# Hybrid attention encoder: gate units moved between the attentions, two scalings moved to ScalarE, four query buffers, half of each weight residual moved to GpSimd

## The chip, the cores and the metric

The kernel runs on one core of one Trainium2 chip. The metric is the device time of one execution in microseconds (us). Engines are named as in the profile: PE is TensorE's matmul side and PEld its weight load, DVE is VectorE, ACT is ScalarE, POOL is GpSimd, SP is SyncE, which here only issues DMAs.

## The reference

Two layers, each on 512 rows of 1024 numbers in float32:

```python
h = rmsnorm(x, norm_g[l])
proj = h @ w_in[l]                     # 1024 -> 4096 columns: q, k, v, gate of groups A and B
# group A, 8 heads x 64: attention in a window of 8 x 16 grid cells, learned relative bias
# group B, 4 heads, two score maps of 64 each, v of 128:
logits = einsum(q, k) * scale
p = softmax(logits + bias)             # bias: T5 buckets, the same in both layers
attn = p[:, :, 0] - lam * p[:, :, 1]
out = rmsnorm(attn @ v, subln_g) * (1 - lam_init)
# both groups
x = x + concat(out_a * silu(gate_a), out_b * silu(gate_b)) @ w_out[l]
```

A last RMSNorm closes the trunk.

## The kernel before

Every matrix product is computed in split precision. A float32 operand is held as a rounded high half and a residual, both in fp32r, and a product is three matmuls: high by high, high by low, low by high. The normalised activations stay resident as `hTh` and `hTl` (transposed, 1024 by 512).

Weights come in units of 256 columns: 24 input units per layer, then four output units. `load_unit` (L86) brings a unit in two halves of 512 KB over SP (L83), casts each half to `wh` on ACT (L98, 128x1024) and takes the residual `wl = raw - wh` in two instructions on DVE (L101, 128x512 each). The pool `wp` has two buffers of `wh` and of `wl`. When a unit is taken, the next one is converted, so the residual of unit n+1 goes into the buffer that the last matmul of unit n-1 frees.

The unit kinds are: V (`proj_tm`, L222, four PSUM tiles of 256 columns), Q (`proj_qk`, one PSUM tile of 512 columns for q, one for k), and G (`gates`, two PSUM tiles of 512 columns), each for group A or B: VB0-1, VA0-1, QB0-3, QA0-3, GB0-1, GA0-1. `evac_q` (L226) turns a q tile into two `qs` tiles (ACT L231, DVE L232), `evac_k` (L237) writes `kt` (ACT L245, DVE L246) and mirrors it to the other 64 partitions by a DMA (L247). A gate tile gives `th` on ACT (L252) and `u` on DVE (L254), and POOL multiplies it into `y` (L483).

AB0-3 are the attentions of group B (`attn_b`): for each of four row blocks two score tiles `st` (PE L271, L272), bias and minimum on DVE (L274), exp on ACT (L277), 1/z (L281, L282), two scalings (L283, L284), four transposes (L288), the split into `pth` and `ptl` (ACT L163, DVE L164), and for each pair of blocks twelve value matmuls (L293). Its tail squares and sums (L297 to L304), takes `row` from PSUM (DVE L306), and goes on POOL and its DMA queue through `ms`, `rs_d` and `rb` to the last product (L308 to L315). AA0-3 are those of group A, two heads each (`attn_a`): `st` (L325), L331 on DVE, exp L334 on ACT, 1/z L336, scaling L337, two transposes (L340), the split, eight value matmuls (L347), and L353, L354.

Three things tie these together. PSUM pools are small: three projection tiles `pp`, two `st`, two `pt`, one `pv`. Some SBUF buffers are shared by tag: `th` with `row`, `u` with `rb`, two buffers each. And each engine runs its instructions in one order, which the framework's scheduler fixes when the program is built, from the program order; that in turn is set by the tuple `ORDER` (L32). The output projection (L540) of a layer comes after all 24 units, starts from the `y` tiles of group B split by ACT and DVE (L516, `yTh`, `yTl`), and is followed by the residual sum and the next norm.

Of the kernel before, what the change touches and what calls it, by code (L numbers as in the profile page):

```python
# [27 lines left out]
W4_BUFS = 10  # L28
WARM = (7, 2)
WRAW_BUFS = 2  # L30
QK_BUFS = 2
ORDER = ("VB0", "QB0", "AB0", "QB1", "VB1", "AB1", "QB2", "AB2", "QB3", "AB3", "VA0", "QA0", "AA0",  # L32
         "QA1", "AA1", "VA1", "QA2", "AA2", "QA3", "AA3", "GB0", "GB1", "GA0", "GA1")
A_TILES = ((0, 1), (1, 1), (2, 1), (0, 3))
A_SLOT = ((0, 0, 256), (1, 1, 128), (2, 1, 128), (0, 1, 768))
A_PV = ((1, 0, 128), (3, 256, 128), (0, 0, 384), (2, 128, 128))
# [10 lines left out]
def hybrid_encoder(ctx: ExitStack, tc: tile.TileContext, x, norm_g, w_in, na_rpb,  # L47
# [18 lines left out]
    V, A, G, T = nc.vector, nc.scalar, nc.gpsimd, nc.tensor  # L66
# [14 lines left out]
    def load_raw(src, hf):  # L81
        r = wp.tile([P, 4, 256], F32, name="wraw", bufs=WRAW_BUFS)
        nc.sync.dma_start(out=r.rearrange("p k c -> p (k c)"), in_=src[hf])  # L83
        return r

    def load_unit(src, raws=None, spare=False):  # L86
        if spare:
            wh, wl = (qk.tile([P, 4, S], F32R, name="kt", bufs=2).rearrange("p k (a c) -> p (k a) c", a=2)
                      for _ in range(2))
        else:  # L90
            wh = wp.tile([P, KC, 256], F32R, name="wh")
            wl = wp.tile([P, KC, 256], F32R, name="wl")
# [165 lines left out]
    def attn_b(h, q, k, vt, yb, nlam, sg, yout):  # L258
        pv = ps_v.tile([P, S], F32, name="pv")
        for qp in range(2):  # L260
            pth_v = w4.tile([P, 4, 256], F32R, name="pth", tag="w4k")
            ptl_v = w4.tile([P, 4, 256], F32R, name="ptl", tag="w4k")
            for qi in range(2):
                qt = 2 * qp + qi
                e = w4.tile([P, 2, S], F32, name="w4k")
                mn = small.tile([P, 2], F32, name="mn")
                z = small.tile([P, 2], F32, name="z")
                for m in range(2):
                    st = ps_s.tile([P, S], F32, name="st")
                    kh, kl = k[m]  # L270
                    T.matmul(out=st, lhsT=q[m][:, qt * P:(qt + 1) * P], rhs=kh, start=True, stop=False)  # L271
                    T.matmul(out=st, lhsT=q[m][:, qt * P:(qt + 1) * P], rhs=kl, start=False, stop=True)  # L272
                    lt = work.tile([P, S], F32, name="lt", bufs=2)
                    V.tensor_tensor_reduce(out=lt, in0=st, in1=yb[:, 48 - 16 * qt:560 - 16 * qt],  # L274
                                           scale=-1.0, scalar=3e38, op0=ALU.add, op1=ALU.min,
                                           accum_out=mn[:, m:m + 1])
                    A.activation(out=e[:, m, :].rearrange("p (b r c) -> p b r c", r=ROWS, c=C8),  # L277
                                 in_=lt.rearrange("p (r b c) -> p b r c", r=ROWS, c=C8),
                                 func=AF.Exp, bias=mn[:, m:m + 1], scale=-1.0, accum_out=z[:, m:m + 1])
                rz = small.tile([P, 2], F32, name="rz")  # L280
                V.reciprocal(out=rz, in_=z)  # L281
                V.tensor_scalar_mul(rz[:, 1:2], rz[:, 1:2], nlam)  # L282
                V.tensor_scalar_mul(e[:, 0, :], e[:, 0, :], rz[:, 0:1])  # L283
                V.scalar_tensor_tensor(out=e[:, 0, :], in0=e[:, 1, :], scalar=rz[:, 1:2], in1=e[:, 0, :],  # L284
                                       op0=ALU.mult, op1=ALU.add)
                pt = ps_t.tile([P, 4, P], F32, name="pt")
                for kt in range(4):
                    T.transpose(out=pt[:, kt, :], in_=e[:, 0, kt * P:(kt + 1) * P], identity=ident)  # L288
                split(pt, pth_v[:, :, qi * P:(qi + 1) * P], ptl_v[:, :, qi * P:(qi + 1) * P])
            n = 0  # L290
            for kt in range(4):
                for vs, pp in ((0, pth_v), (0, ptl_v), (1, pth_v)):
                    T.matmul(out=pv[:, qp * 256:(qp + 1) * 256], lhsT=vt[:, kt, h % 2, vs, :], rhs=pp[:, kt, :],  # L293
                             start=(n == 0), stop=(n == 11))
                    n += 1
# [22 lines left out]
    def attn_a(l, hd, half, q, k, vt, s_out):  # L318
# [3 lines left out]
        for j, (k0, dk) in enumerate(A_TILES):  # L322
            st = ps_s.tile([P, S], F32, name="st")
            for i in range(2):
                T.matmul(out=st[:, 0:256], lhsT=q[:, j * P:(j + 1) * P],  # L325
                         rhs=k[i].rearrange("p (t c) -> p t c", c=P)[:, k0:k0 + dk + 1:dk, :],
                         start=(i == 0), stop=(i == 1))
            e = work.tile([P, 256], F32, name="ea", bufs=3)
            mn = small.tile([P, 1], F32, name="mna")
            i0 = (0, 4, 4, 8)[j]  # L330
            V.tensor_tensor_reduce(out=e, in0=st[:, 0:256],  # L331
                                   in1=ba[:, 64 * i0:64 * i0 + 256],
                                   scale=-1.0, scalar=3e38, op0=ALU.add, op1=ALU.min, accum_out=mn)
            A.activation(out=e, in_=e, func=AF.Exp, bias=mn, scale=-1.0, accum_out=z[:, j:j + 1])  # L334
            rz = small.tile([P, 1], F32, name="rza")
            V.reciprocal(out=rz, in_=z[:, j:j + 1])  # L336
            V.tensor_scalar_mul(e, e, rz)  # L337
            pt = ps_t.tile([P, 4, P], F32, name="pt")
            for i in range(2):
                T.transpose(out=pt[:, i, :], in_=e[:, i * P:(i + 1) * P], identity=ident)  # L340
            t0, sl, stp = A_SLOT[j]
            oh, ol = (_view(p, t0 * 256 + sl * P, [[stp, 2], [1, P]]) for p in ptt)
            split(pt[:, 0:2, :], oh, ol)
# [64 lines left out]
    kh = [hTh[:, i] for i in range(KC)]  # L408
# [48 lines left out]
    for l in range(DEPTH):  # L457
# [223 lines left out]
```

## Time and profile before

| | |
|---|---|
| median of 3 runs | 631.58 us (631.32 to 632.37) |
| profiled execution | 631.53 us, span 629.8 us, mean granted PE clock 0.977 |
| PE busy | 594.4 us (94%) |
| DVE busy | 427.0 us (68%) |
| ACT busy | 320.2 us (51%) |
| POOL busy | 73.6 us (12%) |

All rows come from the profiled execution. PE is busy nearly all the time, so the time is PE's work plus the stretches in which PE idles or runs at a lower clock. A table of busy time by stretch finds these; the timeline of PE and of DVE in such a stretch tells what PE waited for and what stood ahead of it.

### The profile page before, as it was taken

The numbers are of one execution on the slowest core, as the hardware profiler recorded it, in microseconds if no ns is written. First come the engines' busy times: TensorE is split into PE (matmuls) and PEld (weight loads), VectorE is DVE, ScalarE is ACT, GpSimd is POOL, SyncE is SP. The second block draws the span as 40 slices with busy tenths as digits, with TensorE's granted clock in tenths as the row PEclk, the third lists the DMA queues.
The fourth block names the chain that finished last, engine by engine and source line by source line (L and its number), as shares of the span: only waits on it lengthen the run. The fifth ranks groups of instructions, "written<-read, shape, count | busy, mean of one in ns | idle before, by whom it ended". The sixth has DMA issues, their size and how long they took to land.

```text
span 629.8 us, 9006 instructions
## 1 busy us (share of the span) xinstructions
PE 594.4 (94%) x3230; PEld 504.5 (80%) x3230; DVE 427.0 (68%) x1011; ACT 320.2 (51%) x672; POOL 73.6 (12%) x91
## 2 busy tenths in 40 slices
PE   9899995899989999999999999688998999999995
PEld 7888883788888888888898798577887888888883
DVE  2755667597887777754674576578788877777263
ACT  5433546374656555734254344635666556664232
POOL 4400000111022002200000000020101200111001
PEclk9999997989999999999999999979999999999998
DMA  6854232313533443453643533320335354226214
GB/s 233 150 187 119 86 101 85 102 47 104 139 93 117 126 137 120 137 176 132 202 134 100 163 91 99 103 68 1 85 100 143 106 154 125 93 68 206 95 67 134
DMA packets 25166, 74.48 MB, mean 118 GB/s; under 512 B 7329, under 2 KB 7329, under 8 KB 24098
## 3 DMA queue, kind: packets, MB, share of 16 engines
q1 hardware_dynamic: 23648, 71.51, 37.6%
q0 software_dynamic: 1472, 2.40, 2.3%
q8 instruction: 26, 0.43, 0.3%
q14 instruction: 18, 0.15, 0.1%
q10 hardware_dynamic: 2, 0.00, 0.0%
HBM read 60.23 MB, written 4.21 MB: 102 GB/s over the span
## 4 chain that ended last, share of the span: by engine, by line
PE 81%; DVE 10%; ACT 5%; issue 3%; POOL 0%; POOLq 0%; DVEq 0%; ACTq 0%
PE pp L210 39%; PE pp L540 11%; PE pp L222 11%; PE pv L293 3%; PE pv L347 2%; PE pt L340 2%; DVE lt L274 2%; DVE wl L101 2%; PE st L325 2%; PE st L271 2%; PE pv L540 2%; PE st L272 2%; PE pt L288 1%; PE pt L195 1%; PE pp L437 1%
## 5 line engine op out<-in xcount | busy, mean ns | idle before, releaser
L101 DVE TENSOR_TENSOR wl<-wraw,wh 128x512 fp32r<-128x512 f32 x148 | 93.5, 686 | 52.6 <-ACT wh L98 20.7
L98 ACT CAST wh<-wraw 128x1024 fp32r<-128x1024 f32 x74 | 74.3, 1048 | 67.4 <-PE pp L210 33.8
L210 PE MATMUL pp<-hTh,wl 128*128 128x512 f32 x384 | 106.1, 399 | 0.0
L210 PE MATMUL pp<-hTh,wh 128*128 128x512 f32 x384 | 102.3, 398 | 0.4 <-DVE kt L246 0.4
L210 PE MATMUL pp<-hTl,wh 128*128 128x512 f32 x384 | 102.6, 396 | 0.0
L210 PEld LDWEIGHTS pp<-hTl,wh 128*128 128x128 f32 x384 | 70.7, 188 | 14.9
L210 PEld LDWEIGHTS pp<-hTh,wh 128*128 128x128 f32 x384 | 69.7, 188 | 14.6 <-PE pt L288 0.9
L210 PEld LDWEIGHTS pp<-hTh,wl 128*128 128x128 f32 x384 | 70.1, 188 | 14.0
L163 ACT CAST pth<-pt 128x256 fp32r<-128x256 f32 (+1 forms) x96 | 42.3, 443 | 70.2 <-PE pt L288 47.5
L222 PE MATMUL pp<-wh,hTh 128*128 128x256 f32 x224 | 66.0, 295 | 7.4 <-DVE v L164 7.0
L164 DVE TENSOR_TENSOR ptl<-pt,pth 128x256 fp32r<-128x256 f32 (+1 forms) x96 | 48.6, 508 | 31.3 <-ACT pth L163 30.6
L222 PE MATMUL pp<-wh,hTl 128*128 128x256 f32 x224 | 65.4, 292 | 0.0
L222 PE MATMUL pp<-wl,hTh 128*128 128x256 f32 x224 | 65.1, 290 | 0.0
L222 PEld LDWEIGHTS pp<-wh,hTh 128*128 128x128 f32 x224 | 44.2, 197 | 10.4 <-DVE v L164 7.9
L277 ACT ACTIVATE w4k<-lt,mn 128x512 f32<-128x512 f32 x64 | 45.9, 721 | 5.4 <-DVE mn L274 5.1
L274 DVE CUSTOM_DVE_ANT_0 lt<-st,yb 128x512 f32<-128x512 f32 x64 | 43.1, 681 | 3.4 <-PE st L272 2.9
L331 DVE CUSTOM_DVE_ANT_0 ea<-st,ba 128x256 f32<-128x256 f32 x64 | 26.4, 419 | 27.3 <-PE pt L340 19.6
L222 PEld LDWEIGHTS pp<-wl,hTh 128*128 128x128 f32 x224 | 44.0, 196 | 0.6
L222 PEld LDWEIGHTS pp<-wh,hTl 128*128 128x128 f32 x224 | 43.9, 196 | 0.5
L271 PE MATMUL st<-kt,qs 128*128 128x512 f32 x64 | 29.1, 454 | 11.0 <-DVE mn L274 9.2
L483 POOL TENSOR_TENSOR y<-y,u 128x512 f32<-128x512 f32 x16 | 21.6, 1348 | 144.7 <-DVE u L254 122.2
L334 ACT ACTIVATE ea<-ea,mna 128x256 f32<-128x256 f32 x64 | 32.7, 513 | 9.7 <-DVE mna L331 8.2
(124 smaller groups left out, 1066.7 us busy)
## 6 DMA issues: line engine op xcount, KB each, us to landing
wraw<-in_w_in_dram SPq DMA_DIRECT2D x64, 512.0 KB, 4.0
kt<-kt SPq DMA_DIRECT2D x16, 512.0 KB, 4.4
wraw<-in_w_out_dram SPq DMA_DIRECT2D x16, 512.0 KB, 3.7
ba<-in_na_rpb_dram SPq DMA_DIRECT2D x16, 384.0 KB, 3.6
y<-in_x_dram SPq DMA_DIRECT2D x8, 512.0 KB, 4.5
yb<-in_t_table_dram SPq DMA_DIRECT2D x8, 280.0 KB, 2.8
rb<-rs_d POOLq DMA_DIRECT2D x8, 256.0 KB, 4.4
xs_d<-y SPq DMA_DIRECT2D x4, 512.0 KB, 4.3
```

The source lines that it names most:

```text
L98: A.copy(out=wh[:, ks, :], in_=r)
L101: V.tensor_tensor(out=wl[:, kh, :], in0=r[:, 2 * i:2 * i + 2, :], in1=wh[:, kh, :].bitcast(F32), op=ALU.subtract)
L163: A.copy(out=oh, in_=ps)
L164: V.tensor_tensor(out=ol, in0=ps, in1=oh.bitcast(F32), op=ALU.subtract)
L210: T.matmul(out=pp, lhsT=a[:, kc, cs], rhs=b[:, kc, c0:c0 + S], start=(n == 0), stop=(n == 3 * KC - 1))
L222: T.matmul(out=pp[:, 0:256], lhsT=a[kc][:, c0:c0 + P], rhs=b[:, kc, :], start=(n == 0), stop=(n == 3 * KC - 1))
L271: T.matmul(out=st, lhsT=q[m][:, qt * P:(qt + 1) * P], rhs=kh, start=True, stop=False)
L274: V.tensor_tensor_reduce(out=lt, in0=st, in1=yb[:, 48 - 16 * qt:560 - 16 * qt], scale=-1.0, scalar=3e38, op0=ALU.add, op1=ALU.min, accum_o ...
L277: A.activation(out=e[:, m, :].rearrange("p (b r c) -> p b r c", r=ROWS, c=C8), in_=lt.rearrange("p (r b c) -> p b r c", r=ROWS, c=C8), fun ...
L331: V.tensor_tensor_reduce(out=e, in0=st[:, 0:256], in1=ba[:, 64 * i0:64 * i0 + 256], scale=-1.0, scalar=3e38, op0=ALU.add, op1=ALU.min, acc ...
L334: A.activation(out=e, in_=e, func=AF.Exp, bias=mn, scale=-1.0, accum_out=z[:, j:j + 1])
L540: T.matmul(out=pp, lhsT=a[k][:, t * P:(t + 1) * P], rhs=b[:, kc, :], start=(half + kc + i == 0), stop=(half == 1 and kc == 3 and i == 2))
```

## The change

Five edits. The number of `qs` buffers goes from two to four. `ORDER` places the gate units GB0, GB1, GA0 and GA1 between the attentions, and VA0 ahead of AB3, VA1 ahead of AA1; before, all four gate units stood at the end, behind AA3. The residual of each weight unit's second half (L101) goes from DVE to POOL. The scalings L283 (128x512) and L337 (128x256) go from DVE to ACT, as an activation Copy with the scale taken from a column.

```diff
-QK_BUFS = 2
-ORDER = ("VB0", "QB0", "AB0", "QB1", "VB1", "AB1", "QB2", "AB2", "QB3", "AB3", "VA0", "QA0", "AA0",
-         "QA1", "AA1", "VA1", "QA2", "AA2", "QA3", "AA3", "GB0", "GB1", "GA0", "GA1")
+QK_BUFS = 4
+ORDER = ("VB0", "QB0", "AB0", "QB1", "VB1", "AB1", "QB2", "GB0", "AB2", "QB3", "VA0", "AB3", "QA0", "GB1",
+         "AA0", "QA1", "VA1", "AA1", "QA2", "AA2", "QA3", "GA0", "AA3", "GA1")
...
-                V.tensor_tensor(out=wl[:, kh, :], in0=r[:, 2 * i:2 * i + 2, :], in1=wh[:, kh, :].bitcast(F32),
+                (G if hf else V).tensor_tensor(out=wl[:, kh, :], in0=r[:, 2 * i:2 * i + 2, :], in1=wh[:, kh, :].bitcast(F32),
                                 op=ALU.subtract)
...
-                V.tensor_scalar_mul(e[:, 0, :], e[:, 0, :], rz[:, 0:1])
+                A.activation(out=e[:, 0, :], in_=e[:, 0, :], func=AF.Copy, scale=rz[:, 0:1])
...
-            V.tensor_scalar_mul(e, e, rz)
+            A.activation(out=e, in_=e, func=AF.Copy, scale=rz)
```

The edits move instructions on every engine. On DVE at the end of QB3, layer 0, before the change, the first residual of the next unit (QA0's, which waits for PE) stands ahead of group B's attention:

```order
L164 TENSOR_TENSOR ptl<-pt,pth 128x4x128 [waits Activation_49]
L101 TENSOR_TENSOR wl<-wraw,wh 128x512 [waits DMAHW2_49,PE_49,Activation_49]
L101 TENSOR_TENSOR wl<-wraw,wh 128x512
L101 TENSOR_TENSOR wl<-wraw,wh 128x512 [waits DMAHW3_49,Activation_49]
L101 TENSOR_TENSOR wl<-wraw,wh 128x512
L299 TENSOR_TENSOR sq<-sq,su 64x512 [waits Activation_49]
L164 TENSOR_TENSOR ptl<-pt,pth 128x4x128 [waits Activation_49]
L274 ISA lt,mn<-st,yb 128x512 [waits Activation_49]
```

The same place on DVE after the change:

```order
L303 TENSOR_TENSOR sr<-sq,sr 64x512 [waits Activation_49]
L284 SCALAR_TENSOR_TENSOR w4k<-w4k,rz 128x512 [waits DVE_49,Activation_49]
L101 TENSOR_TENSOR wl<-wraw,wh 128x512 [waits DMAHW6_49,PE_49,Activation_49]
L101 TENSOR_TENSOR wl<-wraw,wh 128x512
L306 TENSOR_SCALAR row<-pv 1x512 [waits PE_49]
L246 TENSOR_TENSOR kt<-pp,kt 64x8x8x8 [waits Activation_49]
L164 TENSOR_TENSOR ptl<-pt,pth 128x4x128 [waits Activation_49] x2
```

The waiting residual still stands there, now two instructions long, with `row`, the k evacuation and two splits behind it, and no score tile.

PE at the same place, before: after the last matmuls of QB3's k product come score tiles that wait for DVE, and VA0's first product behind them.

```order
L210 MATMUL pp<-hTh,wl 128x512 x3
L271 MATMUL st<-kt,qs 128x512 [waits DVE_49]
L272 MATMUL st<-kt,qs 128x512
L271 MATMUL st<-kt,qs 128x512 [waits DVE_49]
L272 MATMUL st<-kt,qs 128x512
L304 MATMUL pv<-sr,ones_r 2x512 [waits DVE_49]
L288 MATMUL pt<-ident,w4k 128x128 [waits DVE_49,PE_49]
L288 MATMUL pt<-ident,w4k 128x128 x3
L271 MATMUL st<-kt,qs 128x512 [waits DMAHW4_49,DVE_49]
L272 MATMUL st<-kt,qs 128x512
L293 MATMUL pv<-pth,v 128x256 [waits DVE_49,Activation_49]
```

And PE there after the change, from the score tiles ahead of the k product to VA0's first product (L222):

```order
L271 MATMUL st<-kt,qs 128x512 [waits DVE_49]
L272 MATMUL st<-kt,qs 128x512
L210 MATMUL pp<-hTh,wh 128x512 [waits DVE_49,PE_49]
L210 MATMUL pp<-hTh,wh 128x512 x7
L210 MATMUL pp<-hTl,wh 128x512 x8
L210 MATMUL pp<-hTh,wl 128x512 x8
L288 MATMUL pt<-ident,w4k 128x128 [waits DVE_49]
L288 MATMUL pt<-ident,w4k 128x128 x3
L304 MATMUL pv<-sr,ones_r 2x512 [waits DVE_49]
L288 MATMUL pt<-ident,w4k 128x128 [waits DVE_49,PE_49]
L288 MATMUL pt<-ident,w4k 128x128 x3
L293 MATMUL pv<-pth,v 128x256 [waits DVE_49,Activation_49]
```

The score tiles moved ahead of the k product, which now itself waits for DVE; the value matmuls of the next head wait for DVE and ACT, and VA0 follows them.

On PE at the end of layer 0 before the change, the last attention work lies between matmuls of the last gate unit (L210), up to the output projection (L540):

```order
L210 MATMUL pp<-hTl,wh 128x512 x8
L210 MATMUL pp<-hTh,wl 128x512 x4
L347 MATMUL pv<-pth,v 128x256 [waits DVE_49,Activation_49]
L210 MATMUL pp<-hTh,wl 128x512
L347 MATMUL pv<-ptl,v 128x256 [waits DVE_49]
L210 MATMUL pp<-hTh,wl 128x512
L340 MATMUL pt<-ident,ea 128x128 [waits DVE_49,PE_49]
L340 MATMUL pt<-ident,ea 128x128
L210 MATMUL pp<-hTh,wl 128x512 x2
L540 MATMUL pp<-wh,yTh 128x512
```

After it, the last gate unit is done while a good part of AA3 is still to come. The first 12 of the rows between its last matmul and the output projection:

```order
L210 MATMUL pp<-hTh,wl 128x512 x2
L325 MATMUL st<-kt,qs 128x256 [waits DVE_49]
L325 MATMUL st<-kt,qs 128x256
L340 MATMUL pt<-ident,ea 128x128 [waits DVE_49,PE_49]
L340 MATMUL pt<-ident,ea 128x128
L325 MATMUL st<-kt,qs 128x256 [waits DVE_49]
L325 MATMUL st<-kt,qs 128x256
L347 MATMUL pv<-pth,v 128x256 [waits Activation_49]
L347 MATMUL pv<-ptl,v 128x256 [waits DVE_49]
L347 MATMUL pv<-pth,v 128x2x128
L347 MATMUL pv<-ptl,v 128x2x128
L347 MATMUL pv<-pth,v 128x256
```

They go on in this manner: 38 matmuls in all (10 of L325, 14 of L340, 14 of L347) lie between the last gate matmul and the first of the output projection, and none of a projection is among them. ACT has 19 instructions there from the last gate's `th` to the first cast of `yTh`: one L252, five L163 of `pth`, five L334, six L337, one L353, one L163 of `yTh`.

ACT at the end of that stretch after the change; the scalings L337 stand among the exps (L334) and the splits (L163), and the two casts at the end are the first that the output projection needs:

```order
L337 ACTIVATE ea<-ea,rza 128x256 [waits DVE_49]
L163 CAST pth<-pt 128x2x128 [waits PE_49]
L337 ACTIVATE ea<-ea,rza 128x256 [waits DVE_49]
L334 ACTIVATE ea,za<-ea,mna 128x256 [waits DVE_49]
L163 CAST pth<-pt 128x2x128 [waits PE_49]
L334 ACTIVATE ea,za<-ea,mna 128x256 [waits DVE_49,Activation_49]
L337 ACTIVATE ea<-ea,rza 128x256 [waits DVE_49]
L163 CAST yTh<-y 128x512 x2
```

What moved: AA3's chain of exp, scaling and split lies wholly on ACT now, and ahead of the casts of `yTh`.

## Rows read from the trace of the kernel before

**Rows 1.** The page, busy time by engine.

```profile
PE 594.4 (94%) x3230; PEld 504.5 (80%) x3230; DVE 427.0 (68%) x1011; ACT 320.2 (51%) x672; POOL 73.6 (12%) x91
```

**Rows 2.** By stretch: busy us of PE, PEld, DVE, ACT, POOL; PEclk, DMA share, GB/s.

```profile
97.00:131.00 34.00, 24.45 (x132) 19.98 (x131) 25.59 (x61) 18.81 (x43) 4.18 (x5) 0.80 0.31 86
400.00:434.00 34.00, 24.09 (x141) 19.61 (x140) 24.51 (x56) 18.35 (x41) 4.07 (x5) 0.85 0.23 63
160.00:192.00 32.00, 29.67 (x204) 26.48 (x203) 27.36 (x75) 20.70 (x50) 5.39 (x7) 1.00 0.42 109
464.00:496.00 32.00, 29.64 (x202) 26.60 (x202) 28.02 (x77) 20.71 (x51) 5.00 (x7) 1.00 0.38 100
200.00:400.00 200.00, 199.75 (x1060) 169.85 (x1060) 127.78 (x290) 95.17 (x193) 14.29 (x13) 1.00 0.43 132
102.70:112.60 9.90, 7.42 (x24) 5.26 (x25) 8.45 (x18) 3.53 (x8) 2.36 (x3) 0.50 0.20 59
126.60:129.60 3.00, 3.00 (x14) 3.00 (x15) 2.93 (x9) 2.71 (x7) 0.00 (x0) 0.50 0.00 0
406.70:416.40 9.70, 7.45 (x22) 5.04 (x23) 8.89 (x20) 4.12 (x9) 2.24 (x3) 0.50 0.23 75
```

**Rows 3.** PE's timeline: start, length, engine, instruction, [idle before <-releaser].

```profile
96.56 0.95 PE L210 MATMUL pp<-hTh,wl 128*128 128x512 f32 x3
101.96 0.50 PE L271 MATMUL st<-kt,qs 128*128 128x512 f32 x1 [4.45 <-DVE mn L274]
...
126.56 0.58 PE L222 MATMUL pp<-wh,hTh 128*128 128x256 f32 x1 [2.35 <-DVE v L164]
...
182.23 0.39 PE L222 MATMUL pp<-wh,hTh 128*128 128x256 f32 x1 [1.13 <-DVE v L164]
...
235.11 2.02 PE L210 MATMUL pp<-hTl,wh 128*128 128x512 f32 x8
236.96 0.39 PE L210 MATMUL pp<-hTh,wl 128*128 128x512 f32 x1
...
431.42 0.38 PE L222 MATMUL pp<-wh,hTh 128*128 128x256 f32 x1 [2.36 <-DVE v L164]
```

**Rows 4.** DVE's timeline, the end of QB3 and the tail of AB2, layer 0.

```profile
97.61 2.50 DVE L101 TENSOR_TENSOR wl<-wraw,wh 128x512 fp32r<-128x512 f32 x4 [6.79 <-ACT sq L297]
...
106.62 0.68 DVE L306 TENSOR_SCALAR row<-pv 1x512 f32<-1x512 f32 x1
```

**Rows 5.** Groups by line and shape: busy us, mean ns | idle before.

```profile
L101 DVE TENSOR_TENSOR wl<-wraw,wh 128x512 fp32r<-128x512 f32 x148 | 93.5, 686 | 52.6 <-ACT wh L98 20.7 <-PE pp L210 17.2 <-issue 7.1
L334 ACT ACTIVATE ea<-ea,mna 128x256 f32<-128x256 f32 x64 | 32.7, 513 | 9.7 <-DVE mna L331 8.2
L337 DVE TENSOR_SCALAR ea<-ea,rza 128x256 f32<-128x256 f32 x64 | 25.7, 402 | 1.4
L163 ACT CAST pth<-pt 128x256 fp32r<-128x256 f32 x64 | 23.8, 372 | 22.5 <-PE pt L340 22.0
L232 DVE SCALAR_TENSOR_TENSOR qs<-pp,qs 64x512 fp32r<-64x512 f32 x32 | 22.1, 689 | 4.8 <-ACT qs L231 3.9
L483 POOL TENSOR_TENSOR y<-y,u 128x512 f32<-128x512 f32 x16 | 21.6, 1348 | 144.7 <-DVE u L254 122.2 <-DVE y L354 22.5
L231 ACT ACTIVATE qs<-pp 64x512 fp32r<-64x512 f32 x32 | 19.0, 593 | 28.9 <-DVE qs L232 13.7 <-PE st L325 8.7 <-PE pp L210 4.4
L283 DVE TENSOR_SCALAR w4k<-w4k,rz 128x512 f32<-128x512 f32 x32 | 16.1, 504 | 0.0
```

**Rows 6.** The page, DMA issues: KB, us to landing.

```profile
kt<-kt SPq DMA_DIRECT2D x16, 512.0 KB, 4.4
```

**Rows 7.** POOL's timeline: the end of AB2's tail, and a gate product of layer 0.

```profile
119.49 1.28 POOL L315 TENSOR_TENSOR y<-y,rb 128x512 f32<-128x512 f32 x1 [5.80 <-ACT w4k L277]
...
265.18 1.68 POOL L483 TENSOR_TENSOR y<-y,u 128x512 f32<-128x512 f32 x1 [7.76 <-DVE u L254]
```

**Rows 8.** DVE's timeline beside that gate product.

```profile
265.69 1.72 DVE L164 TENSOR_TENSOR yTl<-y,yTh 128x512 fp32r<-128x512 f32 x1
```

## The prediction

> **What bounds the kernel now.** The busy times come first [rows 1]: PE works 594.4 of 629.8 us, DVE 427.0, ACT 320.2 and POOL 73.6. So PE sets the time, and what can be won is where it idles or is slow. The table by stretch comes second [rows 2]. Between 200 and 400 us PE is busy for 199.75 of 200.00; there is nothing to win there. Around 97 to 131 us it is busy for 24.45 of 34.00 (9.55 idle), at 400 to 434 us, the same place in layer 1, for 24.09 (9.91 idle), and from 160 and from 464 us on for 29.67 and 29.64 of 32.00 (2.33 and 2.36 idle). In three stretches the granted clock is 0.50, which is the lower level: there 7.42, 3.00 and 7.45 us of PE work took twice as long as at the full level, a loss of 3.71 + 1.50 + 3.73 = 8.94 us. All of it together is 9.55 + 9.91 + 2.33 + 2.36 + 8.94 = 33.09 us.
>
> The timelines come third. PE ends QB3's k product at 97.51 and next waits 4.45 us for a score tile that DVE must first empty [rows 3]. DVE had itself been idle for 6.79 us before its four residuals L101 at 97.61 [rows 4]: they need the `wl` buffer that this k product was still reading, and all of AB2 stood behind them in DVE's order. It is a circle of two engines in fixed order: PE waits for DVE, DVE had waited for PE. The clock is lower from 102.70 on, after that gap.
>
> **The change, part by part.**
>
> *Durations.* From row to row one matmul of 512 columns takes (236.96 - 235.11) / 8 = 0.23 us [rows 3]; I take 0.12 for 256 columns and 0.09 for a transpose. DVE's evacuations of 512 columns are taken at L232's 0.69, ACT's of 512 at L231's 0.59, its splits of 256 at 0.37, its exps at 0.51 [rows 5].
>
> *Scalings to ACT.* DVE loses 16.1 + 25.7 us (L283, L337) [rows 5]. No row shows a Copy with a column scale of this width on ACT: L337 there lies between the split's 0.37 and the exp's 0.51, and I take 0.51, since it reads and writes SBUF as the exp does; L283, twice as wide, lies between 0.59 and 1.03, and I take 0.7. ACT gets 64 x 0.51 + 32 x 0.7 = 55 us, for some 375 in all. Away from the places below this lies beside PE's matmuls.
>
> *Residuals to POOL.* Of 156 instructions L101 (148, and 8 into `kt` buffers) half go: DVE loses 78 x 0.63 = 49 us (0.63 from four in 2.50 us [rows 4]), POOL gets 78 x 1.35 = 105 (L483, the same shape [rows 5]). A pair is ready 2.7 us after its cast. In POOL's order some pairs stand behind waits of the `rb` chain, but a unit is converted a whole unit (48 matmuls of 0.23, some 11 us) before its use, so I count nothing.
>
> *Query buffers.* Two more `qs` buffers cost no time; they let a q product be emptied while the attention before it still reads the older pair.
>
> *The order.* All four holes of [rows 2] go, with their clock: -33.09. The score tiles of the attention in flight now stand ahead of QB3's k product and not behind it. What is late next I get by walking through the new order with the durations above, per layer:
>
> (a) QB3 to AB3, 5.2 us. Both PSUM tiles of GB0 stay occupied until `th` and `u` find their shared buffers free (`row` and `rb` of AB0 and AB1 hold these), so one `pp` is left. QB3's k product must wait for both q evacuations: 0.59 on ACT, five DVE instructions of 0.69 and four short ones (0.6 together, my estimate) are 4.65, beside 3.65 of PE work (four transposes, eight score matmuls, twelve of 0.12): 1.0. After the k product the next `pv` waits for `row`, which on DVE stands behind two residuals that wait for this very product: 0.25 + 1.25 + 0.68 = 2.2 against 0.95 of transposes and L304: 1.2. Its second matmul waits for a k evacuation and a split, 2 x 0.69: 1.3. VA0's first tile waits for the second k evacuation: 0.5. AB3's score waits for `kt`, 4.4 us to landing [rows 6], against 24 x 0.12 and four transposes, 3.2: 1.2.
>
> (b) AA0 and QA1, 2.8 us. From the end of QA1's q product to its k product ACT runs four L334 and L337 (2.05), two L231 and one L252 (1.77), one split (0.37), and DVE one L232 (0.69): 4.9, against some 2.1 of PE work. The scaling on ACT is one of the links.
>
> (c) The end of AA3, 5.2 us. Before, gate units covered it: PE had no gap. Now PE has 38 matmuls between the last gate and the output projection: 24 x 0.12 + 14 x 0.09 = 4.1. ACT has nineteen instructions: L252, L353 and the first `yTh` at 0.59 each, five splits at 0.37, five exps and six scalings at 0.51: 9.3. With scalings at 0.37 it is 8.4.
>
> (d) GB1's second `u` waits until `rb` of AB3 is used up. In AB2's case that took from 107.30 (end of `row` [rows 4]) to 120.77 (end of L315 [rows 7]), 13.5, and 0.7 for `u` itself; VA1's second tile, which needs this `pp`, comes 13.2 after (10.7 of PE work and most of (b)). I take half of the 1.0, 0.5.
>
> The start, AA1, AA2, the output projection and the tail stay as they are. *Sum:* 631.53 (the profiled execution, span 629.8 and 1.7 around it; 0.05 from the median shown) - 33.09 + 2 x (5.2 + 2.8 + 5.2 + 0.5) = 625.8 us.
>
> A price on the residuals is open. At 265.18 POOL starts a product of two SBUF tiles beside a DVE residual of two SBUF tiles: POOL takes 1.68 instead of 1.35, and DVE's next such residual 1.72 [rows 7, 8] instead of 0.69, a delay of 1.03. That rate per encounter is the upper bound; the lower is nothing, where DVE reads PSUM or waits anyway. The Trainium skill, "SBUF — State Buffer", "Who interferes with whom", speaks against this edit: a VectorE instruction with two SBUF inputs and a GpSimd instruction that reads SBUF lock each other out for a whole instruction, and both residuals are of this kind. The 1.72 agrees with it. By it every crossing costs DVE up to one POOL instruction, and the time is that of the second rival below.
>
> **The rivals.**
>
> 1. Slower: the clock falls in the new holes. The three stretches at 0.50 cost 8.94, or 3.0 each on average (1.5 to 3.7). If it falls at (a) and at (c) in both layers, that is 4 x 3.0 = 12, and 637.7 us; it takes from three falls on (634.7) to be slower than now, two give 631.8. For it: (c) leaves PE busy for only 44% of 9.3 us, and a gap of 2.35 at 126.56 was followed by the lower clock. Against it: one of 2.36 at 431.42 and one of 1.13 at 182.23 were not [rows 2, 3], and no single gap that I find is over 1.3.
>
> 2. No change: DVE and POOL meet on the path. Two crossings per layer, the residuals ahead of `row` in (a) and a combination L284 in AB2 or AB3, at 1.03 make 4.1, and 629.9; with one clock fall 632.9.
>
> 3. Much faster: the chains of (a), (b), (d) lie beside work that my walk does not see, since it lets each instruction start only when the last one ahead of it has ended. Only (c), which is a plain count of ACT's work, remains: 631.53 - 33.09 + 10.4 = 608.8. For it: in the layer's middle DVE works 127.78 and ACT 95.17 of 200 us without a PE gap [rows 2]. Against it: one free `pp` is not seen there before.
>
> 4. It does not do what it says: the residual that waits for PE still stands in DVE's order at QB3's end. If score tiles are behind it again in some other place, one hole of 9.7 and its clock loss come back: 625.8 + 13 = 639. I find none in the order.
>
> **How the numbers follow.** My forecast, 625.8 with up to ten less and four more, has a chance of 0.42; rival 3 has 0.15; rival 2 and one or two clock falls, within 0.2% (1.3 us, about what a measurement of this kernel can tell from no change), 0.13; rival 1, and the rest of rivals 2 and 4, 0.30. So faster 0.57, same 0.13, slower 0.30. The range goes from near rival 3 to near rival 1, 610 to 638; the likeliest case alone would be 616 to 630.
>
> **What would show it.** Right: no PE gap of 4.45 at the end of QB3 and none of 2.35 in VA0; a gap of some 5 us in pieces just ahead of the first L540 with ACT busy all through it; PE waiting for `row` and for `kt` around VA0; L337 on ACT near 0.5; ACT near 375 us, DVE near 335, POOL near 180. Wrong: a second or third stretch at 0.50 (rival 1), L101 on DVE well over 0.69 on average (rival 2), or PE nearly without gaps at VA0 and AA0 (rival 3).

## The result, and the profile after

The changed kernel takes 634.48 us (median of 11 runs, 632.72 to 637.11) against 631.54 us before (11 runs): ratio 1.0051, 95% interval 1.0031 to 1.0071. It is slower by half a per cent; 625.8 was forecast, faster. The profiled execution takes 632.72 us, with a span of 630.9 and a mean granted clock of 0.978, against 631.53, 629.8 and 0.977 [rows 1]. Its busy times:

```profile
PE 597.9 (95%) x3230; PEld 507.3 (80%) x3230; DVE 371.6 (59%) x837; ACT 367.7 (58%) x768; POOL 192.0 (30%) x169
```

The load moved in the direction that was meant (DVE 427.0 to 371.6, ACT 320.2 to 367.7, POOL 73.6 to 192.0). The time did not follow, since PE's idle time only changed its place. The table by stretch of the changed kernel (columns as in [rows 2]): first the six stretches with large gaps, then the parts of them in which the granted clock is at its lower level.

```profile
119.00:132.00 13.00, 9.80 (x59) 8.56 (x58) 7.53 (x14) 6.75 (x14) 5.47 (x5) 0.87 0.62 188
176.00:187.00 11.00, 8.85 (x40) 6.58 (x39) 8.82 (x29) 10.35 (x30) 2.22 (x3) 0.84 0.35 101
258.00:272.00 14.00, 11.73 (x56) 9.25 (x55) 10.04 (x33) 12.26 (x33) 4.64 (x3) 0.76 0.39 127
422.00:433.00 11.00, 8.15 (x48) 7.21 (x47) 7.12 (x11) 6.87 (x13) 4.72 (x4) 0.84 0.51 143
480.00:501.00 21.00, 16.23 (x90) 13.49 (x89) 12.63 (x36) 15.77 (x38) 5.54 (x5) 0.92 0.40 115
566.00:580.00 14.00, 10.96 (x54) 8.23 (x53) 11.53 (x34) 12.68 (x37) 4.64 (x3) 0.88 0.26 82
125.30:128.30 3.00, 3.00 (x14) 3.00 (x15) 0.58 (x1) 0.60 (x1) 1.04 (x1) 0.50 0.87 256
183.20:186.10 2.90, 2.47 (x7) 2.00 (x8) 2.07 (x6) 2.88 (x10) 1.61 (x2) 0.50 0.13 23
265.10:271.70 6.60, 6.37 (x25) 4.64 (x23) 4.55 (x20) 6.32 (x20) 1.28 (x1) 0.50 0.71 236
428.80:432.20 3.40, 3.40 (x18) 3.29 (x17) 1.16 (x2) 0.43 (x2) 0.09 (x1) 0.50 0.92 252
497.20:500.60 3.40, 3.40 (x17) 3.29 (x16) 1.66 (x4) 0.73 (x3) 0.86 (x2) 0.51 0.89 219
575.70:579.10 3.40, 3.40 (x12) 2.51 (x12) 2.47 (x6) 3.35 (x9) 0.00 (x0) 0.51 0.00 0
```

Idle in the first six: 3.20 + 2.15 + 2.27 + 2.85 + 4.77 + 3.04 = 18.28 us; three gaps elsewhere that the kernel before did not have (1.30, 1.34 and 0.86) add 3.5, in all 21.8, against 24.15 in the four stretches of [rows 2]. Lost to the lower clock in the last six: half of 22.04 busy us, 11.0, against 8.94 before. Before, the clock fell three times, after two gaps of 4.45 and one of 2.35; now it falls six times, after gaps of some 2 us or several short ones. PE's timeline at some of the largest gaps:

```profile
122.53 0.36 PE L293 MATMUL pv<-pth,v 128*128 128x256 f32 x1 [2.10 <-DVE row L306]
...
123.63 0.39 PE L293 MATMUL pv<-ptl,v 128*128 128x256 f32 x1 [0.75 <-DVE ptl L164]
...
183.63 0.69 PE L340 MATMUL pt<-ident,ea 128*128 128x128 f32 x2 [1.07 <-ACT ea L337]
...
263.93 0.38 PE L347 MATMUL pv<-ptl,v 128*128 128x256 f32 x1 [2.04 <-DVE ptl L164]
...
319.19 0.66 PE L195 MATMUL pt<-ident,xn 128*128 128x128 f32 x4 [1.34 <-DVE hTl L164]
...
496.91 0.56 PE L340 MATMUL pt<-ident,ea 128*128 128x128 f32 x2 [1.35 <-ACT ea L337]
```

The gaps of 4.45 us of [rows 3] are gone. In four of these rows, at three places, PE waits for DVE, and each time a pair of residuals stands ahead of what PE wants. DVE's timeline at these places (in the second a reciprocal lies between the two residuals):

```profile
119.42 2.37 DVE L101 TENSOR_TENSOR wl<-wraw,wh 128x512 fp32r<-128x512 f32 x2 [0.75 <-ACT wh L98]
...
261.18 0.69 DVE L101 TENSOR_TENSOR wl<-wraw,wh 128x512 fp32r<-128x512 f32 x1 [0.20 <-ACT ea L334]
...
261.86 1.68 DVE L101 TENSOR_TENSOR wl<-wraw,wh 128x512 fp32r<-128x512 f32 x1
...
316.15 2.38 DVE L101 TENSOR_TENSOR wl<-wraw,wh 128x512 fp32r<-128x512 f32 x2
```

And POOL's, beside them:

```profile
119.62 1.61 POOL L101 TENSOR_TENSOR wl<-wraw,wh 128x512 fp32r<-128x512 f32 x1 [5.55 <-ACT wh L98]
...
261.32 1.68 POOL L101 TENSOR_TENSOR wl<-wraw,wh 128x512 fp32r<-128x512 f32 x1 [9.29 <-ACT ea L334]
...
316.20 1.78 POOL L101 TENSOR_TENSOR wl<-wraw,wh 128x512 fp32r<-128x512 f32 x1 [1.42 <-ACT wh L98]
```

Both halves of one unit are converted at the same time, one on DVE and one on POOL; such a meeting is called a crossing below. A pair on DVE then takes 2.4 us instead of 1.25. The groups by line say it for the whole run, where [rows 5] had 686 ns:

```profile
L101 POOL TENSOR_TENSOR wl<-wraw,wh 128x512 fp32r<-128x512 f32 x74 | 114.6, 1569 | 236.2 <-ACT wh L98 146.5 <-ACT pth L163 23.2 <-ACT ea L334 18.6
L101 DVE TENSOR_TENSOR wl<-wraw,wh 128x512 fp32r<-128x512 f32 x74 | 71.0, 998 | 48.2 <-ACT wh L98 32.6 <-PE pp L210 14.8 <-ACT ea L334 0.4
L337 ACT ACTIVATE ea<-ea,rza 128x256 f32<-128x256 f32 x64 | 31.0, 504 | 5.2 <-DVE rza L336 5.1
```

### The profile page after: what moved, and what is told of

Read it like the earlier page. It is cut to its first block, busy times and chain, and to the rows that moved or that the text cites. A ratio compares the mean times of both kernels' runs of the same rounds, so it can differ in the third digit from the quotient of the medians.

```text
span 630.9 us, 9031 instructions
## 1 busy us (share of the span) xinstructions
PE 597.9 (95%) x3230; PEld 507.3 (80%) x3230; DVE 371.6 (59%) x837; ACT 367.7 (58%) x768; POOL 192.0 (30%) x169
## 4 chain that ended last, share of the span: by engine, by line
PE 40%; DVE 3%; issue 3%; DMA 2%; ACT 2%; POOL 1%; POOLq 0%; DVEq 0%; ACTq 0%; SPq 0%
PE pp L210 19%; PE pp L222 7%; PE pp L540 5%; DMA kt<-kt 2%; PE pv L293 1%; DVE wl L101 1%; PE pv L347 1%; PE st L271 1%; PE st L272 1%; PE pt L340 1%; PE pv L540 1%; PE pt L288 1%; PE st L325 1%; DMA wraw<-in_w_in_dram 1%; DVE ptl L164 0%
## 5 line engine op out<-in xcount | busy, mean ns | idle before, releaser
L101 POOL TENSOR_TENSOR wl<-wraw,wh 128x512 fp32r<-128x512 f32 x74 | 114.6, 1569 | 236.2 <-ACT wh L98 146.5
L210 PE MATMUL pp<-hTh,wl 128*128 128x512 f32 x384 | 104.7, 397 | 0.0
L210 PE MATMUL pp<-hTh,wh 128*128 128x512 f32 x384 | 103.2, 400 | 0.8 <-DVE qs L232 0.8
L210 PE MATMUL pp<-hTl,wh 128*128 128x512 f32 x384 | 102.0, 396 | 0.0
L101 DVE TENSOR_TENSOR wl<-wraw,wh 128x512 fp32r<-128x512 f32 x74 | 71.0, 998 | 48.2 <-ACT wh L98 32.6
L210 PEld LDWEIGHTS pp<-hTh,wh 128*128 128x128 f32 x384 | 70.4, 190 | 15.9 <-PE st L272 1.2
L210 PEld LDWEIGHTS pp<-hTl,wh 128*128 128x128 f32 x384 | 70.9, 188 | 15.2
L210 PEld LDWEIGHTS pp<-hTh,wl 128*128 128x128 f32 x384 | 70.6, 188 | 14.5
L222 PE MATMUL pp<-wh,hTl 128*128 128x256 f32 x224 | 65.2, 291 | 0.0
L222 PE MATMUL pp<-wh,hTh 128*128 128x256 f32 x224 | 65.2, 291 | 0.1
L222 PE MATMUL pp<-wl,hTh 128*128 128x256 f32 x224 | 65.0, 291 | 0.0
L163 ACT CAST pth<-pt 128x256 fp32r<-128x256 f32 (+1 forms) x96 | 41.7, 440 | 38.1 <-PE pt L288 25.4
L222 PEld LDWEIGHTS pp<-wh,hTh 128*128 128x128 f32 x224 | 44.3, 198 | 1.2 <-DVE kt L246 0.3
L222 PEld LDWEIGHTS pp<-wl,hTh 128*128 128x128 f32 x224 | 44.2, 197 | 0.7
L222 PEld LDWEIGHTS pp<-wh,hTl 128*128 128x128 f32 x224 | 44.0, 197 | 0.3
L334 ACT ACTIVATE ea<-ea,mna 128x256 f32<-128x256 f32 x64 | 32.5, 508 | 19.4 <-DVE mna L331 19.0
```

Of the source, the lines that this page charges most:

```text
L101: (G if hf else V).tensor_tensor(out=wl[:, kh, :], in0=r[:, 2 * i:2 * i + 2, :], in1=wh[:, kh, :].bitcast(F32), op=ALU.subtract)
L163: A.copy(out=oh, in_=ps)
L210: T.matmul(out=pp, lhsT=a[:, kc, cs], rhs=b[:, kc, c0:c0 + S], start=(n == 0), stop=(n == 3 * KC - 1))
L222: T.matmul(out=pp[:, 0:256], lhsT=a[kc][:, c0:c0 + P], rhs=b[:, kc, :], start=(n == 0), stop=(n == 3 * KC - 1))
```

## The experiments

Sixteen kernels were run. Ratios are to the kernel before, timed beside each of them on the same chip (its median was 631.6 to 633.5). O is the new order, Q the four query buffers, P the residual half on POOL, A the two scalings on ACT; the changed kernel is O+Q+P+A. The kernels ran on different chips, so a difference between two of them in us is good to about 3 us: taken from the ratios instead of the medians, the differences below shift by up to 3 us. O without Q, and P alone, were not run.

**Which edit costs: each undone in turn.** O+Q+A:

```diff
-                (G if hf else V).tensor_tensor(out=wl[:, kh, :], ...
+                V.tensor_tensor(out=wl[:, kh, :], ...
```

> The changed kernel with one edit undone: all residuals L101 are on DVE again; order, four query buffers and both scalings on ACT stay. Theory A (two residuals of SBUF tiles on DVE and POOL hold each other up, DVE's L101 takes 0.998 us there instead of 0.686, and the gaps of 2.04 and 1.34 us behind it start the lower clock): L101 is back at 0.69, the gap of 2.04 at the end of AA3 and that of 1.34 in the output projection go, at least two of the six stretches at clock 0.50 go, and the time falls by 4 to 9 us, to 626 to 630. Theory B (the order itself, with one projection tile left free, makes the gaps and the clock follows): gaps and clock stay, 632 to 636. The residual ahead of `row` at QB3 gets four instructions long (2.5 us) by both, so the gap there stays at about 2.

Measured 629.89 us, ratio 0.9963 (0.9936 to 0.9990), 0.7% under the changed kernel. L101 on DVE is back at 721 ns and the gap at 319 is gone, as theory A said. But gaps of 2.3 and 4.1 us stay at the two ends of AA3, those at QB3 grow to 3.2 and 3.9, and the clock still falls five times and costs 12.8. DVE now has four residuals ahead of what PE wants: 3.58 us at QB3 (from 114.55), where one of them meets POOL's product L315, and 2.50 at the end of AA3 (from 257.13), where POOL does nothing and the clock falls all the same, by 261. Net, the residual half on POOL costs 4.6 us in this order; it is not the cause of the rest.

O+Q+P:

```diff
-                A.activation(out=e[:, 0, :], in_=e[:, 0, :], func=AF.Copy, scale=rz[:, 0:1])
+                V.tensor_scalar_mul(e[:, 0, :], e[:, 0, :], rz[:, 0:1])
...
-            A.activation(out=e, in_=e, func=AF.Copy, scale=rz)
+            V.tensor_scalar_mul(e, e, rz)
```

> The changed kernel with the two scalings L283 and L337 back on DVE; order, query buffers and the residual half on POOL stay. Theory C (ACT's scalings lengthen the chain at the end of AA3 and in AA0, and the gaps there come from them): gaps at AA0 and at the end of AA3 shrink from 2.15 and 2.28 us to about 1 each, 627 to 630. Theory A: the crossings of POOL and DVE residuals stay or grow, since DVE has 42 us more to do, 633 to 638.

Measured 637.23 us, ratio 1.0067 (1.0040 to 1.0094): theory C falls. The gaps at AA0 shrink in layer 0, from 2.15 to 1.0 us, and not in layer 1 (5.5 against 4.77), and the end of AA3 keeps 2.2 and 2.6 us of gap, now behind DVE. Against the changed kernel (1.0051) the difference is not clear of noise.

O+Q, both edits above undone:

> The kernel before with the new order and four query buffers only; residuals and scalings all on DVE. Theory A: without the crossings the order alone gives the gain that was forecast for it, 624 to 629. Theory B: the order alone is as slow as the whole change, 632 to 637. If DVE's load (427 us) is what limits the new places, the gap at QB3 is over 3 us.

Measured 643.76 us, ratio 1.0177 (1.0138 to 1.0216). Gaps of 6.0 us stand at QB3 in both layers, so the new order does not cure that place. Both theories miss: the order loses more than either allowed, 38 us against four query buffers alone (605.65, below).

Q+P+A, the tuple `ORDER` of the kernel before:

> The changed kernel with the old order: residual half on POOL, scalings on ACT and four query buffers stay. The circle at QB3's end (PE waits for DVE's score tile, DVE's residuals wait for PE) is in the old order, so both theories expect the gaps of 4.45 us there. Theory A: new crossings add 1 to 3 us of gaps, 631 to 636. Theory B: two DVE instructions less in the circle and 91 us less on DVE shorten it by 1 to 2 us per layer, 626 to 630.

Measured 599.36 us, ratio 0.9453 (0.9410 to 0.9497). Both theories had the old gaps of 4.45 us come back, and both were wrong: PE has no gap at all there. By stretch, the place of [rows 2]'s first two rows:

```profile
90.00:124.00 34.00, 34.00 (x223) 30.50 (x222) 29.20 (x63) 25.51 (x51) 9.50 (x9) 1.00 0.46 128
384.00:418.00 34.00, 34.00 (x221) 30.45 (x220) 28.84 (x61) 25.21 (x52) 10.86 (x11) 1.00 0.31 95
```

So the new order costs 35 us beside the other three edits, and these three give 32 of the kernel before's time back.

**What cures the old order.** Q alone, one line:

```diff
-QK_BUFS = 2
+QK_BUFS = 4
```

> The kernel before with one edit: four query buffers. Theory Q (two buffers were the lock at QB3: its q tile could not be emptied while AB2's later score tiles still read the older pair, so k's product and the score tiles fell behind each other): the gaps of 4.45 us and their clock go, 605 to 614. Theory L (DVE's load is the lock, 427 us, and the run with the old order is quick because 91 us of it went to ACT and POOL): 626 to 632, gaps of over 3 us stay at QB3.

Measured 605.65 us, ratio 0.9578 (0.9532 to 0.9625): theory Q. DVE's load is what it was (424.7 us), but the circle is open. DVE's timeline at QB3's end:

```profile
94.59 0.69 DVE L232 SCALAR_TENSOR_TENSOR qs<-pp,qs 64x512 fp32r<-64x512 f32 x1
...
97.48 0.69 DVE L232 SCALAR_TENSOR_TENSOR qs<-pp,qs 64x512 fp32r<-64x512 f32 x1
98.21 2.50 DVE L101 TENSOR_TENSOR wl<-wraw,wh 128x512 fp32r<-128x512 f32 x4
```

And the same place in the kernel before:

```profile
105.91 0.68 DVE L232 SCALAR_TENSOR_TENSOR qs<-pp,qs 64x512 fp32r<-64x512 f32 x1
```

Here DVE takes the two halves of QB3's q tile from 94.59 and 97.48 on, and PE ends the k product at 98.09; in the kernel before it took the first half 8.4 us after the k product's end (105.91 against 97.51) and the second from 108.45 on. The four residuals, still ahead of other work, start without a wait, since DVE comes to them busy. The edit also gave the engines another order: VA0's product follows the k product at once, at 97.92, where before it began at 110.22, behind the score tiles.

A alone, the reverse of the diff of O+Q+P on the kernel before:

> The kernel before with one edit: both scalings on ACT, 42 us less on DVE. Theory Q: the gaps at QB3 stay over 3 us, 625 to 632. Theory L: they shrink with DVE's load, 612 to 622.

Measured 630.29 us, ratio 0.9960 (0.9933 to 0.9987): single gaps of 4.24 and 4.22 us stay at QB3. So 42 us less on DVE do not open the circle.

**Where the order loses.** On Q+P+A (599 us), one move at a time. First the V units:

```diff
-... "QB3", "AB3", "VA0", "QA0", "AA0", "QA1", "AA1", "VA1", "QA2", ...
+... "QB3", "VA0", "AB3", "QA0", "AA0", "QA1", "VA1", "AA1", "QA2", ...
```

> The run with the old order (599 us), with VA0 ahead of AB3 and VA1 ahead of AA1 as in the changed kernel, gates all at the end. Theory G (the gate units alone cost): 597 to 601. Theory V (the V units, placed ahead of an attention, no longer lie beside it and AB3 or AA1 lie bare later): 603 to 608.

Measured 598.52 us, ratio 0.9468 (0.9422 to 0.9514): no cost. GB0 behind QB2:

```diff
-... "QB2", "AB2", ..., "AA3", "GB0", "GB1", "GA0", "GA1"
+... "QB2", "GB0", "AB2", ..., "AA3", "GB1", "GA0", "GA1"
```

> The run with the old order (599 us), with one gate unit GB0 moved from the end to behind QB2, as in the changed kernel. Theory G1 (a gate between group B's attentions holds two projection tiles until `th` and `u` are free of `row` and `rb`, and all that follows goes through one tile): new gaps of 2 to 3 us around VA0 in each layer and the clock falling after them, 607 to 613. Theory G2 (the loss comes at the end of AA3, from the cover that the gates gave there): three gate units still cover AA3, no change, 598 to 601.

Measured 618.02 us, ratio 0.9764 (0.9700 to 0.9829): 18.7 us for one unit, more than either theory allowed. ACT's timeline, layer 1:

```profile
426.93 0.60 ACT L252 ACTIVATE th<-pp 128x512 f32<-128x512 f32 x1 [5.66 <-DMA ms<-row]
```

ACT stands for 5.66 us at the gate's `th`: its buffer is still read as `row` by the `ms` DMA, which POOL issued at 419.14, behind a pair of residuals. Every ACT instruction behind it waits too. But PE's largest gaps in this run end with something else. PE's timeline, and DVE's ahead of the first gap:

```profile
261.38 0.58 PE L347 MATMUL pv<-ptl,v 128*128 128x256 f32 x1 [2.35 <-DVE ptl L164]
...
418.80 0.36 PE L293 MATMUL pv<-pth,v 128*128 128x256 f32 x1 [2.09 <-DVE row L306]
...
427.96 0.50 PE L271 MATMUL st<-kt,qs 128*128 128x512 f32 x1 [2.85 <-DMA kt<-kt]
```

```profile
415.69 2.37 DVE L101 TENSOR_TENSOR wl<-wraw,wh 128x512 fp32r<-128x512 f32 x2 [0.77 <-ACT wh L98]
417.98 0.67 DVE L306 TENSOR_SCALAR row<-pv 1x512 f32<-1x512 f32 x1
```

The gap of 2.09, with one of 0.75 behind it and the same two in layer 0, waits for `row`, which stands behind a pair of residuals in a crossing, as in the changed kernel. The gap of 2.85 ends with the `kt` DMA, which SP issued at 421.56, after a k evacuation that ACT's wait did not hold up, and which landed at 427.91, 6.35 us later. The gaps of 2.35 at 261 and of 1.69 at 562.87 lie at the two ends of AA3: three gate units no longer cover it. GB1 behind QA0:

```diff
-... "QA0", "AA0", ..., "AA3", "GB0", "GB1", "GA0", "GA1"
+... "QA0", "GB1", "AA0", ..., "AA3", "GB0", "GA0", "GA1"
```

> The run with the old order (599 us), with one gate unit GB1 moved from the end to behind QA0, as in the changed kernel. By theory S its second `u` waits for `rb` of AB3 and its `th` for `row`, and AA0 and QA1 run through one projection tile: gaps of 2 to 3 us there, 604 to 610. If only GB0 meets the shared buffers: 598 to 601.

Measured 622.43 us, ratio 0.9832 (0.9799 to 0.9866): 23 us. ACT has the same wait, and PE's gaps beside it again end with `row` and with the `kt` DMA:

```profile
182.87 0.60 ACT L252 ACTIVATE th<-pp 128x512 f32<-128x512 f32 x1 [3.48 <-DMA ms<-row]
```

```profile
176.02 0.38 PE L347 MATMUL pv<-pth,v 128*128 128x256 f32 x1 [3.12 <-DVE row L306]
...
185.19 0.74 PE L325 MATMUL st<-kt,qs 128*128 128x256 f32 x4 [2.07 <-DMA kt<-kt]
```

`row` stands behind a pair of residuals here too (2.36 us, from 172.32 on), and this `kt` DMA was issued at 178.14, before ACT's wait began. The end of AA3 has a gap of 2.12 us in both layers.

Three gate units ahead of AA3, one behind it:

```diff
-... "QA3", "AA3", "GB0", "GB1", "GA0", "GA1"
+... "QA3", "GB0", "GB1", "GA0", "AA3", "GA1"
```

> The run with the old order (599 us), with GB0, GB1 and GA0 placed ahead of AA3, so that only GA1 follows it. Theory G2: the end of AA3 lies bare, gaps of 2 to 3 us and a clock fall in each layer as in the changed kernel, 608 to 614. Theory G1: the buffers of `row` and `rb` are long free by then, no gaps at VA0, 598 to 602.

Measured 609.67 us, ratio 0.9639 (0.9582 to 0.9697): 10.3 us. Theory G2 is right here: the end of AA3 lies bare. PE's timeline there, layer 0:

```profile
255.31 0.39 PE L347 MATMUL pv<-pth,v 128*128 128x256 f32 x1 [0.89 <-ACT pth L163]
...
256.66 0.41 PE L340 MATMUL pt<-ident,ea 128*128 128x128 f32 x2 [0.96 <-DVE ptl L164]
...
257.90 0.38 PE L347 MATMUL pv<-ptl,v 128*128 128x256 f32 x1 [0.83 <-DVE ptl L164]
```

**Whether the shared buffers are the price.** On the run with GB0 moved, and on the changed kernel:

```diff
-W4_BUFS = 10
+W4_BUFS = 8
...
-        row = work.tile([1, S], F32, name="row", tag="th", bufs=2)
+        row = work.tile([1, S], F32, name="row", bufs=2)
...
-        rb = work.tile([P, S], F32, name="rb", tag="u", bufs=2)
+        rb = work.tile([P, S], F32, name="rb", bufs=2)
```

> The run with GB0 behind QB2 (618 us), with `row` and `rb` in buffers of their own and no longer in those of `th` and `u` (the room is taken from two of the ten 4 KB buffers). Theory S (the shared buffers are the price: ACT stands 5.66 us at the gate's `th` until the `ms` DMA has read `row`, and DVE at `u`): the gap of 2.85 us before AB3 and most of the 18 us go, 600 to 606. Theory T (the gate's place itself is the price, or the smaller pool costs as much): 612 to 619.

Measured 619.90 us, ratio 0.9819 (0.9775 to 0.9863), no gain in time. But the gaps at VA0 are gone: PE is busy for 17.97 of 18.00 us from 112 on and for all of 20.00 from 410 on, where it had 14.43 of 18.00 and 14.25 of 20.00 with shared buffers. Three gaps, 5.45 us together, stand in the output projection instead.

> The changed kernel with `row` and `rb` in buffers of their own (two of the ten 4 KB buffers less). Theory S: the gaps at QB3 and AA0 shrink, 620 to 628; the end of AA3 stays bare, some 10 us. Theory T: 632 to 638.

Measured 618.96 us, ratio 0.9799 (0.9753 to 0.9845), 2.4% under the changed kernel and below theory S's range. By stretch: QB3, AA0, the end of AA3, the output projection.

```profile
116.00:130.00 14.00, 14.00 (x117) 13.79 (x116) 9.64 (x18) 7.27 (x16) 4.10 (x4) 1.00 0.64 190
172.00:184.00 12.00, 12.00 (x93) 11.45 (x92) 8.49 (x22) 9.71 (x24) 4.08 (x3) 1.00 0.47 122
244.00:258.00 14.00, 11.84 (x56) 9.46 (x55) 11.40 (x33) 12.72 (x34) 4.60 (x3) 0.76 0.46 136
300.00:313.00 13.00, 7.86 (x44) 6.79 (x43) 10.34 (x16) 3.70 (x7) 3.60 (x3) 0.74 0.41 139
```

The first two gaps are filled with the tuple `ORDER` unchanged, but PE's order is another: where the changed kernel runs QB3's k product as one block of 24 matmuls (from 113.51 on) and then waits, this one has it in pieces between score tiles, with VA0's product right behind it (from 114.41 on). The third gap stays as forecast; the fourth is new. A control, the run with the old order and only the smaller pool:

> A control: the run with the old order (599 us) with eight of the ten 4 KB buffers and nothing else. If the smaller pool is what kept the runs with own buffers near 619, the gaps of 5.1 to 5.5 us in the output projection of layer 0 (PE waits for DVE's norm, L189 and L164) and the clock fall behind them appear here too, 605 to 612. If they come from the gate's place, 599 to 602.

Measured 612.61 us, ratio 0.9669 (0.9637 to 0.9702), 13.3 us more than with ten buffers, and the gaps are there. PE's timeline in the output projection:

```profile
304.37 0.66 PE L195 MATMUL pt<-ident,xn 128*128 128x128 f32 x4 [1.48 <-DVE xn L189]
306.04 1.12 PE L195 MATMUL pt<-ident,xn 128*128 128x128 f32 x4 [1.01 <-DVE xn L189]
...
309.89 1.12 PE L195 MATMUL pt<-ident,xn 128*128 128x128 f32 x4 [2.30 <-DVE hTl L164]
```

So the smaller pool explains the new gaps. They are 4.8 us of its price; another 7.7 lie behind PE's last matmul, which ends 15.5 us before the end of the span where it was 7.8 with ten buffers. If the price of 13 us simply adds, own buffers alone would save, as an estimate, some 11 us with GB0 moved and nearly 29 on the changed kernel; that was not run, for want of room. Only `row` given its own buffer (W4_BUFS 9):

> The run with GB0 behind QB2 (618 us), with only `row` in a buffer of its own (one of the ten 4 KB buffers less); `rb` still shares with `u`. Theory S1 (`row`, through ACT's wait at `th`, is the price): the gap of 2.85 us before AB3 goes, 607 to 613. Theory S2 (`rb`, through DVE's wait at `u`, is the price): 615 to 620, PE waits at VA0's later tiles.

Measured 616.76 us, ratio 0.9748 (0.9699 to 0.9797). ACT no longer waits for the `ms` DMA, and the gap before AB3 falls from 2.85 to 1.61, but the one at `pv`, 2.8, stays, and the time is the same within noise (615.15 to 620.25 against 612.79 to 619.90). So ACT's wait at `th` is not what the 18.7 us are paid for, unless the pool, one smaller here, costs as much; the output projection and the end show no such price (a gap of 0.86 and 7.8 us, as with GB0 moved). What `rb` weighs is left open.

**The other two edits on the old order.** Q+A:

> The run with the old order (599 us), with all residuals back on DVE: four query buffers and the scalings on ACT. Theory A on the old order (the crossings of the residuals cost PE time wherever they are): gaps of 1.5 us before AB1 go, 595 to 598, and this is the best version. Theory N (without gaps nobody waits for DVE, the residual's engine doesn't matter): 599 to 602.

Measured 617.37 us, ratio 0.9769 (0.9736 to 0.9802). Both theories miss: gaps of 4.4 and 3.7 us in all at QB3 are back, and DVE empties QB3's q tile late again (from 103.26 and 106.80 on, in a stretch where PE ended the k product at 94.4). So four buffers allow the early evacuation but do not bring it about; the order of the instructions decides. Q+P:

> The run with the old order (599 us), with the scalings back on DVE: four query buffers and the residual half on POOL. If the four buffers carry the gain and the two moves from DVE only trim it, 598 to 606; if, as with the other move alone (617), one move without the other makes a worse order on DVE, 610 to 620.

Measured 593.13 us, ratio 0.9365 (0.9338 to 0.9392): the fastest of all. PE's largest wait in it (us in total, times, longest):

```profile
PE st L271 <- DMA kt<-kt: 2.2, 1, 2.2
```

Outside the start, the rest is waits for `kt` of 0.7 and 0.6 us in total. L101 on DVE takes 980 ns here too, and PE never waits for it: the same crossings that hurt in the new order cost nothing where PE has work. Beside Q, P saves 12.5 us (605.65 to 593.13) and A costs 11.7 (617.37); with P, A costs 6.2 (599.36). Of P's 12.5, 6.3 are idle time of PE; the rest is PE's busy time and the trace does not explain it.

## Why the prediction was wrong

The direction was wrong (chance given to slower: 0.30); the time lies inside the range of 610 to 638.

The step that failed is in the sum: "All four holes of [rows 2] go, with their clock: -33.09", with the new gaps then added at full clock. The first half held: the old gaps went. But the new ones, forecast at 2 x 13.7 = 27.4 us and measured at 21.8, brought the lower clock with them, 11.0 us that my forecast had at nothing. With both measured terms the sum is 631.53 - 33.09 + 21.8 + 11.0 = 631.2, and PE's busy time without the clock's share is 1.6 us longer (586.4 against 584.8), which gives 632.8 for a profiled 632.72. The gaps' error of 5.6 hides half of the clock's: the forecast missed by less than its worst term.

That is rival 1. Its price was off: six falls of 1.84 each on average, where I had 3.0 each and four. I held against it that "no single gap that I find is over 1.3"; there were two of 2.04 and two of 2.10. All four rest on rival 2, a pair of residuals that DVE needs 2.4 us for while POOL converts the other half: I had the pair ahead of `row` at 1.25 and the wait at 1.2. So at these four places the crossing lengthened the gap, and the clock fell later, 1 to 6 us on. It is not the only way to a fall: with no residual on POOL (O+Q+A) it fell five times and cost 12.8. The sign that I named for rival 2 came too: L101 at 998 ns against 686, and DVE at 371.6 us where I had near 335. The Trainium skill's rule that a VectorE instruction with two SBUF inputs and a GpSimd instruction that reads SBUF shut each other out ("SBUF — State Buffer", "Who interferes with whom") agrees with these durations.

Place by place: (a) was forecast at 5.2 per layer and is 3.20 and 2.85; the wait for `row` came, those of VA0's first tile and of AB3 for `kt` did not. (b) with (d) was put at 3.3, and is 2.15 and 4.77, near in the sum by luck. (c) was put at 5.2, and is 2.27 and 3.04, with ACT busy through it as said, and a further 3.2 and 1.7 lost to the clock behind it. But its mechanism was off: the largest gap there, 2.04 in both layers, waits for DVE's `ptl` behind a pair of residuals and not for ACT, and with the scalings back on DVE the gaps stay. L337 on ACT takes 504 ns and L283 719, as taken. Two gaps of 1.3 us (before AB1 and in the output projection) were not forecast.

A second step was wrong without showing in the sum: the cure of the holes was put to the order, and "Two more `qs` buffers cost no time" was all that the buffers were given. The buffers alone give 26 us; the order with them (O+Q) has gaps of 6.0 us at QB3 and takes 35 to 38 us away. I had seen two prices of the order, the tiles of GB0 held by `th` and `u`, and the bare end of AA3, but sized them against a gain that was not the order's.

Where the order loses is shown: 18.7 us for GB0, 23 for GB1, 10.3 for three gates ahead of AA3, each alone. They do not add up to 35, since each change gives every engine another order. In the first two PE waits for `row` behind a crossing, for the `kt` DMA, and at the end of AA3. Why a gate between attentions costs so much is shown in part: with buffers of their own for `row` and `rb` the gaps beside it go, in both kernels tried, and the changed kernel gains 15.5 us in spite of the smaller pool; with GB0 alone no time is gained, and `row` alone brought nothing. How much of the price is the sharing, and how much the order that the scheduler makes of it, stays open.

## What to carry to other kernels

Where two engines wait for each other in a circle, first ask which buffer closes it, and run that edit alone before the edits around it; then look at the order that results, since here four buffers opened the circle with three sets of edits and not with Q+A or O+Q. Before a unit of work is moved between two others, list the buffers that it shares by tag with its new neighbours: an engine with one queue stands at the first of them, with all that is behind. That an engine stands does not yet say that PE pays: ask what PE's own gap ends with. And a new gap is priced with the lower clock that may follow it: six falls after gaps of some 2 us or less cost 11.0 us here, three after longer ones had cost 8.94.

## What was not expected of the hardware

The granted clock fell to 0.50 by 183.2, within a gap of only 1.07 us (182.56 to 183.63), with four of 0.17 to 0.47 ahead of it. Before the change one of 1.13 at VA1 was not followed by a fall [rows 3]; in Q+P+A the same gap at the same product was:

```profile
167.73 0.50 PE L222 MATMUL pp<-wh,hTh 128*128 128x256 f32 x1 [1.13 <-DVE v L164]
```

```profile
167.90:171.20 3.30, 3.30 (x16) 3.30 (x17) 2.02 (x7) 2.69 (x9) 0.94 (x1) 0.50 0.02 5
```

So the length of a gap alone did not decide it. PE's busy time without the clock's share differs between kernels with the same 3230 matmuls, from 573.7 us (Q+P) to 587.2 (O+Q+P); what is in these 13.5 us the trace does not show.
